# Cross attention: the sample tokens' steps placed behind products of the next head, and the norm factors' spread placed between the halves of the first gate product

## Chip, cores and metric

The kernel runs on one core of one Trainium2 chip. The metric is the device time of one execution in microseconds (us), the median over the runs of one session.

## The reference, cut to what matters

One layer of a streaming encoder works on 1024 prompt tokens and 64 sample tokens, side by side in one token axis of T = 1088. The part that the change touches is the cross attention, with 4 heads of width 256 and 256 memory tokens, and the step after it:

```python
def cross_attn(x, mk, mv, g_cross, w_cq, w_co):
    q = (rms_norm(x, g_cross) @ w_cq).reshape(B, S, MEM_HEADS, MEM_HD)
    s = jnp.einsum('bqhd,bkhd->bhqk', q, mk) * (MEM_HD ** -0.5)
    p = jax.nn.softmax(s, axis=-1)
    o = jnp.einsum('bhqk,bkhd->bqhd', p, mv)
    return o.reshape(B, S, MEM_HEADS * MEM_HD) @ w_co
# prompt tokens: mk, mv from this call's memory; sample tokens: from a cache
hp = hp + cross_attn(hp, mk, mv, ...);  hs = hs + cross_attn(hs, cache_mem_k, cache_mem_v, ...)
h  = h + (silu(rms_norm(h) @ w_gate) * (rms_norm(h) @ w_up)) @ w_down
```

## The kernel before, in words

Nearly every product is made of three matmuls (`mm3`, lines 157 to 159): both operands are split into a rounded high part and a remainder (`split`: ScalarE casts the high part, line 124, VectorE subtracts, line 125). The tensor engine (PE) works through products of this kind almost without a gap; VectorE (DVE), ScalarE (ACT), GpSimd (POOL) and the DMA queue of SyncE (SP) prepare operands and take results.

The program is written as a list of operations in Python, and a scheduler that estimates durations puts each engine's instructions into a fixed order. `issue_after(x)` holds an operation back until instruction x in that order; `in_order(f)` runs f so that its instructions stand behind the last matmul issued so far. `self.later` is a list of functions that `run_later` empties; `dense`, the helper for one product of a weight unit with a token chunk, calls `run_later` at its end.

`cross_phase` loops over the 4 heads (`attend`). For each head and each of the four token chunks in `CQ` (256, 256, 256 and 320 columns) it makes two query products (`pd<-xc,wq`, 24 matmuls each), scales them by the norm factor (`qf`), splits them (`cqs`), makes the scores (`css`, 12 matmuls), a softmax on DVE and ACT (`small_softmax`; names `cnm`, `cden`, `p`), four transposes (`cpt`), a split of these (`cpT`) and 12 matmuls with the values (`cpo`), whose result is split into the tile `co`. The last chunk holds the 64 sample tokens; their queries go to `qsm`. After the four chunks of a head come the sample tokens' own steps, with the cache's keys `ck` and values `cv`: scores `csss` (line 1355, 2 matmuls, 4 records in the trace), softmax into `ps`, two transposes `cpts` (line 1360), a copy `cpTs` (line 1362) and 4 matmuls `cpos` (line 1366, 8 records in the trace), split into the last 64 columns of `co`. These matmuls and the transposes take plain fp32 operands and are not split into three. PSUM has 3 banks for dense products, 2 for scores (`s`), 1 for transposes (`t`), 2 for `cpo` and `cpos` (`o`); the SBUF tag `t2` has 4 buffers for `mraw`, `qf`, `p`, `ck`, `cv` and `ps`.

`cross_out_phase` then multiplies `co` with `w_co` (`pd<-co,wq`; chunks `CH` of 384, 384 and 320 columns), adds the stored residual (`hx`, line 1394) and keeps sums of squares. At its end the norm factors of two of the three chunks are left to the start of the feed-forward: `self.later` then holds `spread_both` (line 369: 6 fp32 matmuls of a factor row with the identity, then two ACT copies into `rstd_f`, line 372).

The feed-forward begins with `gate_up`. Its first gate product is made by `plain`: four result blocks of 544 columns by 2x128 rows, each of two halves `part(i, t, 0)` and `part(i, t, 1)`, each half 24 matmuls. Three first halves, then `early()` (the last factors' roots), then the three second halves, then `run_later`, then the results are taken by `emit` (which needs `rstd_f`), then both halves of the fourth block. A block holds one of 4 PSUM bank pairs, and so does the spread.

Of the kernel before, what the change touches and what calls it, by code (L numbers as in the profile page):

```python
# [11 lines left out]
F32 = mybir.dt.float32  # L12
# [7 lines left out]
P = 128  # L20
D = 1024
KT = D // P
SEQ = 1024
SMP = 64
T = SEQ + SMP
CH = ((0, 384), (384, 384), (768, 320))
CQ = ((0, 256), (256, 256), (512, 256), (768, 320))
BLK = 256
NBLK = SEQ // BLK
H = 4  # L30
# [79 lines left out]
class Kernel:  # L110
# [132 lines left out]
    def plain(self, w, x, emit, early=None, second=None):  # L243

        ps = {}
        def part(i, t, j):
            if j == 0:
                ps[i, t] = self.bank_pair()
            return self.multiply(ps[i, t], w[i, j], x[f"B{j + 1}{t + 1}"], j == 0, j == 1)

        for i, t in ((0, 0), (1, 0), (0, 1)):
            part(i, t, 0)
        if early is not None:
            with self.tc.issue_after(self.last_mm):
                early()
        emits = [(0, 0), (1, 0), (0, 1)]
        out = []
        for i, t in emits:
            out.append(part(i, t, 1))
            if second is not None and len(out) == 1:  # L260
                second(emit(i, t, out[0], None))
        with self.tc.issue_after(self.last_mm):
            self.run_later()
        for (i, t), o in list(zip(emits, out))[second is not None:]:
            emit(i, t, o, None)
        part(1, 1, 0)
        emit(1, 1, part(1, 1, 1), None)
# [1016 lines left out]
    def cross_phase(self):  # L1284
        nc, tc, io = self.nc, self.tc, self.io
        mm = nc.tensor.matmul
        with ExitStack() as ctx:
            cp = ctx.enter_context(tc.tile_pool(name="cp", bufs=1, reuse_waits="tile"))
            pc = ctx.enter_context(tc.tile_pool(name="pc", bufs=1, reuse_waits="tile", space=PSUM))
            self.norm_psum = lambda name: pc.tile([P, 512], F32, tag="t", name=name)  # L1290
            t2 = lambda name: cp.tile([P, 2, 256], F32, tag="t2", bufs=4, name=name)
            outs = [None] * H

            def small_softmax(ps, rows, units, p):
                nm = cp.tile([P, 2], F32, tag="nm", bufs=2, name="cnm")
                den = cp.tile([P, 2], F32, tag="den", bufs=2, name="cden")
                nc.vector.tensor_reduce(nm[:rows, :units], ps[:rows, :units, :], AX.X, ALU.max)
                nc.vector.tensor_scalar(nm[:rows, :units], nm[:rows, :units], -1.0 / 16, None, ALU.mult)
                for i in range(units):
                    nc.scalar.activation(p[:rows, i, :], ps[:rows, i, :], AF.Exp, bias=nm[:rows, i:i + 1], scale=1.0 / 16,  # L1300
                                         accum_out=den[:rows, i:i + 1])
                nc.vector.reciprocal(den[:rows, :units], den[:rows, :units])
                for i in range(units):
                    nc.vector.tensor_scalar(p[:rows, i, :], p[:rows, i, :], den[:rows, i:i + 1], None, ALU.mult)

            def attend(h):
                us = [self.unit(io["w_cq"][2 * h + i], KT) for i in range(2)]
                hl = []
                for src in (self.d_mk, self.d_mv):
                    raw = t2("mraw")  # L1310
                    self.load(raw, src[h])
                    s = cp.tile([P, 2, 2, 256], F32R, tag=f"m{len(hl)}", bufs=1, name="mkv")
                    self.split(raw, s[:, 0], s[:, 1])
                    hl.append(s)
                mk, mv = hl
                outs[h] = self.ring_tiles(1, 2, "co")
                for c0, n in CQ:
                    ps = [self.dense(us[i], self.xs, c0, n) for i in range(2)]
                    qf = t2("qf")
                    for i in range(2):  # L1320
                        nc.vector.tensor_tensor(out=qf[:, i, :], in0=ps[i][:, :256], in1=self.rstd[:, c0:c0 + 256], op=ALU.mult)
                    qs = cp.tile([P, 2, 2, 256], F32R, tag="qs", bufs=2, name="cqs")
                    self.split(qf, qs[:, 0], qs[:, 1])
                    if n > 256:
                        qsm = cp.tile([P, 2, SMP], F32, tag="qsm", bufs=1, name="qsm")
                        for i in range(2):
                            nc.vector.tensor_tensor(out=qsm[:, i, :], in0=ps[i][:, 256:n], in1=self.rstd[:, SEQ:T], op=ALU.mult)
                    pss = pc.tile([P, 2, 256], F32, tag="s", bufs=2, name="css")
                    for t in range(2):
                        for dt in range(2):  # L1330
                            q = qs[:, :, dt, t * P:(t + 1) * P]
                            self.mm3(pss[:, t, :], q[:, 0], q[:, 1], mk[:, 0, dt, :], mk[:, 1, dt, :], dt == 0, dt == 1)
                    p = t2("p")
                    small_softmax(pss, P, 2, p)
                    pt = pc.tile([P, 2, 256], F32, tag="t", bufs=1, name="cpt")
                    for kt in range(2):
                        for t in range(2):
                            nc.tensor.transpose(pt[:, kt, t * P:(t + 1) * P], p[:, t, kt * P:(kt + 1) * P], self.ident)
                    pT = cp.tile([P, 2, 2, 256], F32R, tag="pT", bufs=1, name="cpT")
                    self.split(pt, pT[:, 0], pT[:, 1])  # L1340
                    po = pc.tile([P, 2, 256], F32, tag="o", bufs=2, name="cpo")
                    for dt in range(2):
                        dd = slice(dt * P, (dt + 1) * P)
                        for kt in range(2):
                            self.mm3(po[:, dt, :], mv[:, 0, kt, dd], mv[:, 1, kt, dd], pT[:, 0, kt, :], pT[:, 1, kt, :],
                                     kt == 0, kt == 1)
                    for dt in range(2):
                        o = outs[h][dt]
                        self.split(po[:, dt, :], o[:, 0, c0:c0 + 256], o[:, 1, c0:c0 + 256])
                ck, cv = t2("ck"), t2("cv")  # L1350
                self.load(ck, io["cmkT"][h])
                self.load(cv, io["cmv"][h])
                pss = pc.tile([P, 2, 256], F32, tag="s", bufs=2, name="csss")
                for dt in range(2):
                    mm(pss[:SMP, 0, :], qsm[:, dt, :], ck[:, dt, :], start=dt == 0, stop=dt == 1)
                p = t2("ps")
                small_softmax(pss, SMP, 1, p)
                pt = pc.tile([P, 2, 256], F32, tag="t", bufs=1, name="cpts")
                for kt in range(2):
                    nc.tensor.transpose(pt[:, kt, :SMP], p[:SMP, 0, kt * P:(kt + 1) * P], self.ident[:SMP, :SMP])  # L1360
                pT = cp.tile([P, 2, SMP], F32, tag="pTs", bufs=1, name="cpTs")
                nc.vector.tensor_copy(pT, pt[:, :, :SMP])
                po = pc.tile([P, 2, 256], F32, tag="o", bufs=2, name="cpos")
                for dt in range(2):
                    for kt in range(2):
                        mm(po[:, dt, :SMP], cv[:, kt, dt * P:(dt + 1) * P], pT[:, kt, :], start=kt == 0, stop=kt == 1)
                for dt in range(2):
                    o = outs[h][dt]
                    self.split(po[:, dt, :SMP], o[:, 0, SEQ:T], o[:, 1, SEQ:T])

            for h in range(H):
                attend(h)
            self.couts = sum(outs, [])
# [219 lines left out]
    def turn(self, name, group):  # L1593

        if name == "T4":
            self.slots["B12"] = self.slots["T4"]
            name = "B12"
        if name[0] == "B":
            self.load_operand(name, group)
# [302 lines left out]
```

## Time and profile before

| | |
|---|---|
| time, median of 3 runs | 2162.29 us (2162.05 to 2165.18) |
| the profiled execution's own time | 2162.52 us |
| its span in the profile | 2160.7 us |
| PE busy | 2134.5 us, 99% of the span |
| DVE, ACT, POOL busy | 1552.6, 874.8, 530.4 us |
| DMA | 290.85 MB, 135 GB/s on average |

A row of the timeline gives an instruction's start and its duration in us, engine, source line, operation, result tile and operands, size, a count when equal ones follow each other, and in brackets the idle time of the engine just before it with what ended it. Matmuls overlap: the time that one takes from the next is the difference of their starts, called its slot here.

### The profile page before, as it was taken

Reading aid. Unit: us, or ns where it says so; the run is one execution under the profiler, and the core shown is the slowest. Engines: PE = TensorE matmul, PEld = TensorE weight load, DVE = VectorE, ACT = ScalarE, POOL = GpSimd, SP = SyncE. Lnnn points to the kernel's source line nnn. Section 1 sums busy time; section 2 is a strip of 40 time slices with the busy share of each in tenths; the row PEclk is TensorE's granted clock in tenths of the full one; section 3 lists DMA queues with packets and bytes.
Section 4 is the critical chain, followed back from the end, with each engine's and each line's share of the span. In section 5 each row is a group of like instructions: output and inputs, shape, how many; then the busy total and the mean of one; then the engine's idle time right before and its main releaser. Section 6 shows DMA issues by size and latency. Waiting matters only on the chain.

```text
span 2160.7 us, 41729 instructions
## 1 busy us (share of the span) xinstructions
PE 2134.5 (99%) x16371; PEld 2082.7 (96%) x16371; DVE 1552.6 (72%) x2912; ACT 874.8 (40%) x1894; POOL 530.4 (25%) x448
## 2 busy tenths in 40 slices
PE   9999999999999999999999999999999999999997
PEld 9999999999999997889999999999999999999997
DVE  8987979776677567656455555677777777777597
ACT  8344434344444356543233333343223222334243
POOL 0000000022343135540000000015565556423531
PEclk9999999999999999999999999999999999999998
DMA  7334444435345485336442122413342332484333
GB/s 262 126 126 123 129 145 134 128 114 160 113 140 190 158 260 184 120 116 207 142 142 78 50 64 68 145 58 105 123 147 91 101 132 82 132 298 158 106 116 113
DMA packets 169893, 290.85 MB, mean 135 GB/s; under 512 B 39266, under 2 KB 96546, under 8 KB 169698
## 3 DMA queue, kind: packets, MB, share of 16 engines
q1 hardware_dynamic: 161666, 269.02, 38.8%
q0 software_dynamic: 3424, 10.82, 1.4%
q10 hardware_dynamic: 4608, 8.36, 1.0%
q8 instruction: 129, 2.11, 0.4%
q14 instruction: 66, 0.54, 0.1%
HBM read 196.97 MB, written 91.16 MB: 133 GB/s over the span
## 4 chain that ended last, share of the span: by engine, by line
PE 85%; DVE 7%; DMA 3%; issue 2%; ACT 2%; POOL 1%; SPq 0%; POOLq 0%; DVEq 0%; ACTq 0%
PE pq L226 17%; PE pq L224 16%; PE pq L223 16%; PE pd L157 8%; PE pd L159 8%; PE pd L158 8%; DVE wq L125 2%; DMA hl<-d_op 1%; PE pss L1005 1%; PE pout L1075 1%; DVE T L125 1%; PE pk L766 1%; PE pp L1051 1%; DVE B L125 1%; PE po L159 1%
## 5 line engine op out<-in xcount | busy, mean ns | idle before, releaser
L124 ACT CAST wq<-raw 128x512 fp32r<-128x512 f32 (+1 forms) x499 | 302.0, 614 | 564.7 <-PE pq L226 220.1
L125 DVE TENSOR_TENSOR wq<-raw,wq 128x512 fp32r<-128x512 f32 (+1 forms) x499 | 426.6, 859 | 137.3 <-ACT wq L124 133.9
L224 PE MATMUL pq<-T,wq 128*128 128x272 f32 x1832 | 492.1, 288 | 0.5 <-DVE T L125 0.5
L223 PE MATMUL pq<-T,wq 128*128 128x272 f32 x1832 | 490.4, 287 | 1.6 <-ACT wq L124 0.6
L224 PE MATMUL pq<-B,wq 128*128 128x272 f32 x1592 | 427.3, 288 | 1.9 <-DVE B L125 1.9
L223 PE MATMUL pq<-B,wq 128*128 128x272 f32 x1592 | 425.6, 287 | 0.2 <-ACT B L124 0.2
L226 PE MATMUL pq<-T,wq 128*128 128x272 f32 x1832 | 382.7, 289 | 1.9 <-DVE wq L125 1.9
L201 POOL TENSOR_TENSOR raw<-raw 128x512 f32<-128x512 f32 (+1 forms) x44 | 62.9, 1429 | 1260.5 <-DVE wq L125 527.6
L223 PEld LDWEIGHTS pq<-T,wq 128*128 128x128 f32 x1832 | 344.3, 188 | 3.2 <-ACT xsq L499 1.2
L224 PEld LDWEIGHTS pq<-T,wq 128*128 128x128 f32 x1832 | 343.9, 188 | 1.5 <-issue 0.7
L226 PE MATMUL pq<-B,wq 128*128 128x272 f32 x1592 | 331.9, 289 | 0.0
L224 PEld LDWEIGHTS pq<-B,wq 128*128 128x128 f32 x1592 | 298.9, 188 | 3.4 <-DVE B L125 3.0
L223 PEld LDWEIGHTS pq<-B,wq 128*128 128x128 f32 x1592 | 298.9, 188 | 0.7 <-ACT B L124 0.4
L226 PEld LDWEIGHTS pq<-T,wq 128*128 128x128 f32 x1832 | 289.6, 189 | 3.6 <-DVE wq L125 2.4
L226 PEld LDWEIGHTS pq<-B,wq 128*128 128x128 f32 x1592 | 251.7, 189 | 0.9 <-issue 0.7
L274 DVE TENSOR_TENSOR u<-pq,u 128x544 f32<-128x544 f32 x177 | 127.1, 718 | 76.0 <-PE pq L226 75.5
L613 DVE TENSOR_TENSOR stage<-pq,u 128x544 f32<-128x544 f32 x112 | 80.1, 717 | 32.5 <-PE pq L226 26.7
L157 PE MATMUL pd<-xc,wq 128*128 128x256 f32 (+1 forms) x256 | 74.5, 291 | 0.0
L159 PE MATMUL pd<-xc,wq 128*128 128x256 f32 (+1 forms) x256 | 74.0, 289 | 0.0
L158 PE MATMUL pd<-xc,wq 128*128 128x256 f32 (+1 forms) x256 | 73.7, 288 | 0.0
L1550 POOL TENSOR_TENSOR stage<-stage,rstd_f 128x544 f32<-128x544 f32 x40 | 63.9, 1608 | 39.1 <-ACT stage L1549 39.1
L204 POOL TENSOR_TENSOR raw<-raw 128x512 f32<-128x512 f32 (+1 forms) x44 | 59.0, 1340 | 53.1 <-DVE wq L125 50.5
(388 smaller groups left out, 4508.9 us busy)
## 6 DMA issues: line engine op xcount, KB each, us to landing
hl<-d_op SPq DMA_DIRECT2D x85, 272.0 KB, 5.3
d_qkv<-stage SPq DMA_DIRECT2D x44, 272.0 KB, 2.3
d_op<-stage SPq DMA_DIRECT2D x44, 272.0 KB, 2.2
d_op<-ht SPq DMA_DIRECT2D x44, 272.0 KB, 3.3
raw<-w_gate SPq DMA_DIRECT2D x22, 512.0 KB, 3.5
raw<-w_up SPq DMA_DIRECT2D x22, 512.0 KB, 5.0
raw<-w_down SPq DMA_DIRECT2D x16, 512.0 KB, 4.8
d_gate<-stage ACTq DMA_DIRECT2D x28, 272.0 KB, 2.8
```

The source lines that it names most:

```text
L124: self.last_cast = self.nc.scalar.copy(hi, src).ins
L125: return self.nc.vector.tensor_tensor(out=lo, in0=src, in1=hi.bitcast(F32), op=ALU.subtract).ins
L157: mm(ps, wh, xh, start=start, stop=False)
L158: mm(ps, wh, xl, start=False, stop=False)
L159: self.last_mm = mm(ps, wl, xh, start=False, stop=stop).ins
L201: tt(out=a11, in0=a11, in1=a21, op=sub)
L223: mm(ps[:, c, :HC], w[:, 0, ks], x[:, 0, cs], start=start, stop=False)
L224: mm(ps[:, c, :HC], w[:, 0, ks], x[:, 1, cs], start=False, stop=False)
L226: self.last_mm = mm(ps[:, c, :HC], w[:, 1, ks], x[:, 0, c * HC:(c + 1) * HC], start=False, stop=stop).ins
L274: add = lambda out, a, b: nc.vector.tensor_tensor(out=out, in0=a, in1=b, op=ALU.add)
L613: nc.vector.tensor_tensor(out=o, in0=ps, in1=sb, op=ALU.add)
L1550: nc.gpsimd.tensor_tensor(out=g, in0=g, in1=r[t], op=ALU.mult)
```

## The change

The sample tokens' steps of a head no longer follow its four chunks. `sample` is called in the chunk that holds the sample tokens, loads `ck` and `cv` into tags of their own with one buffer each (`ps` has one too), and puts the scores into `self.later`; they are issued behind the next dense product, and append the transposes behind the one after it, and those append the products with `cv` behind the third. For heads 0 to 2 these are products of the next head. In the last head the chunk of 320 columns comes first, so that they are products of its own later chunks.

In `plain`, when `early` is given, `run_later` runs after the second of the three second halves, not after the third.

```diff
@@ plain
         for i, t in emits:
             out.append(part(i, t, 1))
+            if early is not None and second is None and len(out) == 2:
+                with self.tc.issue_after(self.last_mm):
+                    self.run_later()
@@ cross_phase
+            def sample(h, qsm):
+                ck, cv, p = (cp.tile([P, 2, 256], F32, tag=t, bufs=1, name=t) for t in ("ck", "cv", "ps"))
+                self.load(ck, io["cmkT"][h])
+                self.load(cv, io["cmv"][h])
+
+                def scores():
+                    pss = pc.tile([P, 2, 256], F32, tag="s", bufs=2, name="csss")
+                    for dt in range(2):
+                        mm(pss[:SMP, 0, :], qsm[:, dt, :], ck[:, dt, :], start=dt == 0, stop=dt == 1)
+                    small_softmax(pss, SMP, 1, p)
+                    behind(turn)
+
+                def turn():
+                    pt = pc.tile([P, 2, 256], F32, tag="t", bufs=1, name="cpts")
+                    for kt in range(2):
+                        nc.tensor.transpose(pt[:, kt, :SMP], p[:SMP, 0, kt * P:(kt + 1) * P], self.ident[:SMP, :SMP])
+                    pT = cp.tile([P, 2, SMP], F32, tag="pTs", bufs=1, name="cpTs")
+                    nc.vector.tensor_copy(pT, pt[:, :, :SMP])
+                    behind(lambda: weigh(pT))
+
+                def weigh(pT):
...
+                behind = lambda f: self.later.append(lambda: self.in_order(f))
+                behind(scores)
@@ attend
-                for c0, n in CQ:
+                for c0, n in CQ if h < H - 1 else CQ[3:] + CQ[:3]:
...
                     if n > 256:
...
+                        sample(h, qsm)
...
-                ck, cv = t2("ck"), t2("cv")
-                self.load(ck, io["cmkT"][h])
-                self.load(cv, io["cmv"][h])
...
```

`weigh` holds the four matmuls with `cv` and the split into `co`; the lines removed at the end of `attend` are the same steps in a row.

In the program's order, first PE where head 0 ends. Before, the transposes and the products with `cv` stand together between the last products with the values (`cpo`) and the next head's query products (`pd<-xc`):

```order
L158 MATMUL cpo<-cpT,mkv 128x256
L159 MATMUL cpo<-cpT,mkv 128x256
L1360 MATMUL cpts<-ident,ps 128x64 x2
L1366 MATMUL cpos<-cpTs,cv 128x64 x4
L157 MATMUL pd<-xc_13007,wq 128x256
```

Now the transposes stand alone, then come other products, and the four matmuls with `cv` are parted by the eleven other matmuls of the next chunk's `cpo`:

```order
L159 MATMUL cpo<-cpT,mkv 128x256
L1324 MATMUL cpts<-ident,ps 128x64 x2
L158 MATMUL pd<-xc_13008,wq 128x256
...
L157 MATMUL cpo<-cpT,mkv 128x256
L1333 MATMUL cpos<-cpTs,cv 128x64 x3
L158 MATMUL cpo<-cpT,mkv 128x256
...
L159 MATMUL cpo<-cpT,mkv 128x256
L1333 MATMUL cpos<-cpTs,cv 128x64
L158 MATMUL pd<-xc_13013,wq 128x256
```

Between the transposes and the first of the products stand more than 50 matmuls of other work; the scores `csss` moved up from between the transposes `cpt` of the head's last chunk to among its scores.

Second, PE where the last head ends (`co0`, `co1` with the highest numbers are this head's two result tiles, `pd_15994` is the first product of the second row block of `w_co`). Before, the sample steps are followed by six matmuls of the first row block's chunk of 320 columns:

```order
L159 MATMUL cpo_15813<-cpT_15810,mkv_15406 128x256
L1360 MATMUL cpts_15845<-ident_63,ps_15837 128x64 x2
L1366 MATMUL cpos_15850<-cpTs_15848,cv_15831 128x64 x4
L157 MATMUL pd_15955<-co0_15409,wq_15888 128x320
L158 MATMUL pd_15955<-co0_15409,wq_15888 128x320
L159 MATMUL pd_15955<-co0_15409,wq_15888 128x320
L157 MATMUL pd_15955<-co1_15410,wq_15888 128x320
L158 MATMUL pd_15955<-co1_15410,wq_15888 128x320
L159 MATMUL pd_15955<-co1_15410,wq_15888 128x320
L157 MATMUL pd_15994<-co0_13962,wq_15986 128x384
```

Now six matmuls of the chunk of columns 384 to 767 stand directly behind the last prompt chunk's `cpo`:

```order
L159 MATMUL cpo_15842<-cpT_15839,mkv_15382 128x256
L157 MATMUL pd_15924<-co0_15385,wq_15888 128x384
L158 MATMUL pd_15924<-co0_15385,wq_15888 128x384
L159 MATMUL pd_15924<-co0_15385,wq_15888 128x384
L157 MATMUL pd_15924<-co1_15386,wq_15888 128x384
L158 MATMUL pd_15924<-co1_15386,wq_15888 128x384
L159 MATMUL pd_15924<-co1_15386,wq_15888 128x384
L157 MATMUL pd_15994<-co0_13962,wq_15986 128x384
```

The sample steps are gone from this place; the six matmuls behind it read a piece of `co` that was now written last.

Third, the loads on SP for heads 0 and 1. Before, the cache's keys and values of head 0 come after two weight loads, and the next head's keys and values (`mraw`) behind them:

```order
L118 DMA mraw<-d_mk 128x512
L118 DMA mraw<-d_mv 128x512
L118 DMA raw<-w_cq 128x1024 x2
L118 DMA ck<-cmkT 128x512
L118 DMA cv<-cmv 128x512
L118 DMA mraw<-d_mk 128x512
L118 DMA mraw<-d_mv 128x512
```

Now head 0's stand ahead of the weight loads, and `ck` of head 1 stands ahead of head 1's `mraw`; having one buffer, it waits there for head 0's `csss`:

```order
L118 DMA mraw<-d_mk 128x512
L118 DMA mraw<-d_mv 128x512
L118 DMA ck<-cmkT 128x512
L118 DMA cv<-cmv 128x512
L118 DMA raw<-w_cq 128x1024 x2
L118 DMA ck<-cmkT 128x512
L118 DMA mraw<-d_mk 128x512
L118 DMA mraw<-d_mv 128x512
L118 DMA cv<-cmv 128x512
```

So a load that head 1 needs for its first scores is queued behind one that waits for PE.

More of the change, by code (lines that the diff above doesn't have):

```diff
@@ L1304, in small_softmax @@
                     nc.vector.tensor_scalar(p[:rows, i, :], p[:rows, i, :], den[:rows, i:i + 1], None, ALU.mult)
+            def sample(h, qsm):
[16 more added lines that the diff above has]
+                def weigh(pT):
+                    po = pc.tile([P, 2, 256], F32, tag="o", bufs=2, name="cpos")
+                    for dt in range(2):
+                        for kt in range(2):
+                            mm(po[:, dt, :SMP], cv[:, kt, dt * P:(dt + 1) * P], pT[:, kt, :], start=kt == 0, stop=kt == 1)
+                    for dt in range(2):
+                        o = outs[h][dt]
+                        self.split(po[:, dt, :SMP], o[:, 0, SEQ:T], o[:, 1, SEQ:T])
+                behind = lambda f: self.later.append(lambda: self.in_order(f))
+                behind(scores)
             def attend(h):
@@ L1349, in attend @@
                         self.split(po[:, dt, :], o[:, 0, c0:c0 + 256], o[:, 1, c0:c0 + 256])
-                ck, cv = t2("ck"), t2("cv")
-                self.load(ck, io["cmkT"][h])
-                self.load(cv, io["cmv"][h])
[L1353 to L1369, printed above, removed]
             for h in range(H):
```

## Prediction

> **What bounds the kernel now.** PE is busy nearly throughout the span (the table above), so only what PE does, or what it waits for, can move the time. I asked first who PE waits for in the cross attention from head 0's last chunk to the first output product, and how much idle time there is:
>
> ```profile
> PE cpos L1366 <- DVE cpTs L1362: 1.7, 4, 0.6
> PE cpo L157 <- ACT cpT L124: 0.7, 1, 0.7
> PE cpo L158 <- DVE cden L1302: 0.3, 1, 0.3
> PE pd L157 <- ACT co L124: 0.3, 1, 0.3
> 1207.00:1346.00 139.00, 135.88 (x1046) 130.92 (x1045) 77.85 (x200) 52.48 (x143) 0.00 (x0) 1.00 0.17 54
> ```
>
> The columns are total, times and longest; in the last row, window, length, then busy time of PE, weight loads, DVE, ACT, POOL, and the granted clock. PE misses 3.1 us of 139, all at the sample steps or right behind them; DVE and ACT are half free and the clock is full. So at most some microseconds of 2162 are on offer. Idle time counts from the modelled end of a matmul; I use slots (start to next start). First the slots where nothing waits:
>
> ```profile
> 1185.73 0.49 PE L1338 MATMUL cpt<-ident,p 128*128 128x128 f32 x3
> 1185.97 0.36 PE L158 MATMUL css<-mkv,cqs 128*128 128x256 f32 x1
> 1186.17 0.28 PE L157 MATMUL pd<-xc,wq 128*128 128x256 f32 x1
> 1186.29 0.28 PE L158 MATMUL pd<-xc,wq 128*128 128x256 f32 x1
> ```
>
> Three transposes take 0.24 us (0.08 each), a 256-column matmul 0.12, but 0.20 as the first one behind plain fp32 work: leaving such a block costs 0.08. I scale 0.12 with the columns: 0.15 for 320, 0.18 for 384.
>
> **Waits that go.** Head 0 is the worst, since no query product stands between its last transposes and `cpo`:
>
> ```profile
> 1214.23 0.55 PE L1338 MATMUL cpt<-ident,p 128*128 128x128 f32 x3
> 1215.51 0.39 PE L157 MATMUL cpo<-cpT,mkv 128*128 128x256 f32 x1 [0.73 <-ACT cpT L124]
> 1216.23 0.39 PE L158 MATMUL cpo<-cpT,mkv 128*128 128x256 f32 x1 [0.34 <-DVE cden L1302]
> 1216.46 0.28 PE L159 MATMUL cpo<-cpT,mkv 128*128 128x256 f32 x1
> 1217.74 0.34 PE L1360 MATMUL cpts<-ident,ps 64*128 64x64 f32 x2
> 1218.65 1.10 PE L1366 MATMUL cpos<-cpTs,cv 128*128 128x64 f32 x8 [0.58 <-DVE cpTs L1362]
> 1219.57 0.36 PE L157 MATMUL pd<-xc,wq 128*128 128x256 f32 x1
> ```
>
> Slots against normal: transposes 1.28 for 0.24 (1.04 lost), first `cpo` 0.72 for 0.20 (0.52), second 0.23 for 0.12 (0.11), `cpts` 0.91 for two transposes, 0.17 (0.74). Sum 2.41 us. The eight `cpos` records take 0.92. Head 1 stands for heads 1 to 3:
>
> ```profile
> 1253.65 0.49 PE L1338 MATMUL cpt<-ident,p 128*128 128x128 f32 x3
> 1254.07 1.08 PE L1355 MATMUL csss<-ck,qsm 128*64 128x256 f32 x4
> 1255.08 0.38 PE L157 MATMUL pd<-xc,wq 128*128 128x256 f32 x1
> 1255.30 0.28 PE L158 MATMUL pd<-xc,wq 128*128 128x256 f32 x1
> 1257.89 0.28 PE L159 MATMUL cpo<-cpT,mkv 128*128 128x256 f32 x1
> 1258.10 0.33 PE L1360 MATMUL cpts<-ident,ps 64*128 64x64 f32 x2
> 1258.81 1.10 PE L1366 MATMUL cpos<-cpTs,cv 128*128 128x64 f32 x8 [0.38 <-DVE cpTs L1362]
> ```
>
> `cpts` takes 0.71 for 0.17: 0.54 lost, three times 1.62. In the new order some 26 matmuls (3 us) stand between `cpt` and `cpo` of head 0, and more than 50 (6 us) between `cpts` and `cpos`, against a wait that is over within 1.3 us of the first transpose. All 4.03 us go.
>
> **What is late next: the end of the last head.**
>
> ```profile
> 1340.74 0.28 PE L159 MATMUL cpo<-cpT,mkv 128*128 128x256 f32 x1
> 1340.95 0.34 PE L1360 MATMUL cpts<-ident,ps 64*128 64x64 f32 x2
> 1341.67 1.10 PE L1366 MATMUL cpos<-cpTs,cv 128*128 128x64 f32 x8 [0.38 <-DVE cpTs L1362]
> 1344.42 0.44 PE L157 MATMUL pd<-co,wq 128*128 128x384 f32 x1
> 1344.70 0.34 PE L158 MATMUL pd<-co,wq 128*128 128x384 f32 x1
> 1342.39 0.42 DVE L125 TENSOR_TENSOR co<-cpo,co 128x256 fp32r<-128x256 f32 x1 [0.44 <-ACT co L124]
> 1343.80 1.08 DVE L1394 TENSOR_TENSOR hx<-pd,hx 128x384 f32<-128x384 f32 x2
> ```
>
> Before, `cpos` (0.92), leaving (0.08) and six matmuls of 320 columns (0.90) would bring the next product to 1343.57; it came at 1344.42, 0.62 after the first `hx` began, which frees its bank, and its slot is 0.28 for 0.18: 0.95 lost. So 4.98 us are lost in all. After, the sample steps are away, but the last prompt chunk's `co` is what the six matmuls read, and in DVE's queue `hx` still stands behind it. The last DVE part of `co` ended 2.07 us after the last `cpo` began (1342.39 + 0.42 - 1340.74); then 0.01 to `hx` and 0.62 from there to PE: the next product comes 2.70 us after that `cpo`, where 0.12 and six times 0.18 would make 1.20. 1.50 and the restart's 0.10 are lost: 1.60. The wait is not removed there, it changes its owner. Net of waits: 4.98 - 1.60 = 3.38 us.
>
> **What the split blocks cost.** Before, `csss` stood against the transposes and `cpts` against `cpos`. Now, by the order, they make 5, 3 and 8 blocks of their own (one `cpts` joins a `cpos`) and head 0's transposes two instead of one: 13 more exits. Behind `csss` the exit is 0.10 (0.22 for 0.12), behind the others 0.08: 1.04 to 1.30, I take 1.17. Entering: before, the transposes ahead of `csss` took 0.42 for 0.25, four times 0.17, and `cpts` was entered at 0.21 for 0.12, four times 0.09: 1.04. After, `cpts` three times 0.09; `csss` from a split product is not in the trace: between 0 (as `cpt`) and 0.17, I take 0.09 as for `cpts`, its nearest row, 64 wide too; `cpos` between 0 and 0.09, I take 0 as for `cpt`, which is also 128 wide. That is 0.72 (0.27 to 1.84): 0.32 less than before (0.77 less to 0.80 more). Cross attention: 3.38 - 1.17 + 0.32 = 2.53 us gained (1.28 to 3.11).
>
> The row behind fp32 work says 0.20 for 0.12. The Trainium skill ("TensorE: Matmul & The Clock Gate", "Step-by-step: what each phase is for") says that PE's queue pulls the next weight load ahead of running matmuls, so that the two overlap. By that rule a block's edge need cost nothing, and this sum would be 3.4 to 4.4; the trace does not agree at these edges, and the row decides.
>
> **The spread in the first gate product.** The fourth block's bank is the one that the spread gives back, through two ACT copies:
>
> ```profile
> 1443.85 0.16 DVE L329 TENSOR_TENSOR rs_r<-rs_r,root 128x3 f32<-128x3 f32 x1
> 1446.13 0.29 PE L223 MATMUL pq<-B,wq 128*128 128x272 f32 x1
> 1449.12 1.50 PE L369 MATMUL pq<-ident,rs_r 128*128 128x128 f32 x12
> 1451.51 0.39 PE L223 MATMUL pq<-b,wq 128*128 128x272 f32 x1 [0.90 <-ACT rstd_f L372]
> 1451.74 0.29 PE L224 MATMUL pq<-b,wq 128*128 128x272 f32 x1
> 1177.75 0.83 PE L361 MATMUL pb<-ident,rs_r 128*128 128x128 f32 x6
> 1178.33 0.36 PE L157 MATMUL css<-mkv,cqs 128*128 128x256 f32 x1
> ```
>
> The third second half starts at 1446.13; the spread now stands there. The factors are ready at 1444.01, so it need not wait, and the half behind it (3 us) covers the copies. Six such matmuls took 0.58 elsewhere, twelve 1.17, and 0.20 with the exit: 1.37 for the 2.62 from 1449.12 to 1451.74. Gain 1.25, at least the idle 0.90. If that cover were gone, the 0.90 would be back. In DVE's queue the remainder of a weight of the up product (line 125) stands some operations later than before; its user on PE comes behind the fourth block and two products of up.
>
> **Moved loads.** `ck` and `cv` have buffers of their own now, and on SP each `ck` waits for the previous head's `csss`, with the next head's `mraw` behind it; `cv` waits for the previous `cpos`. Their users stand 6 us or more behind those in the order, against these landing times (first `mraw`, then `cv`):
>
> ```profile
> DMA to landing us min/median/max: 2.5/2.8/4.2
> DMA to landing us min/median/max: 4.0/4.0/5.6
> ```
>
> 4.2, and a 0.6 us cast, still fit: cost 0. The same matmuls, copies and bytes remain.
>
> **Sum.** 2.53 + 1.25 = 3.78 us (2.2 to 4.4) off the profiled execution's 2162.52 gives 2158.7; its own time is 0.2 above the median 2162.29, so 2158.5 against that. From there on the work hangs on `hx`, as before, so the gain should reach the end.
>
> **Rivals.** (1) The edges are free, since the next weights load behind running matmuls: 4.98 - 1.60 + 1.25 = 4.63, up to 5.67 if the 1.04 of entries before goes too: 2157.7 to 2156.6, taken at 2157.2. This is what the rule of the Trainium skill's page on TensorE, above, would make of the time. For it: the entry of `cpt` costs nothing. Against: every first matmul behind fp32 work in this stage takes 0.20.
>
> (2) The gain is given back downstream, by a chain that had just enough time. DVE, third behind the window's length, is full around the gate product:
>
> ```profile
> 1448.00:1458.00 10.00, 9.10 (x75) 8.91 (x74) 10.00 (x15) 7.17 (x12) 1.81 (x2) 1.00 0.00 0
> ```
>
> If DVE sets the pace there, the 1.25 goes, and half of the rest: 2161.0. Against: PE waits in that window for ACT alone, and DVE's moved operations have later users.
>
> (3) Slower: the next head's keys arrive late, as `mraw` stands behind the waiting `ck`. Three heads can pay. With 6 us between `csss` and the first scores, 0.6 for the cast, and 4.2 to land, there is 1 us to spare; each us beyond costs PE a us per head. To be slower by 0.2% (4.3 us) it has to eat 3.8 as well, 2.7 per head: a landing of 8 us, where the longest here is 5.6. It would then be about 2167.
>
> (4) The change doesn't do what it says: excluded, the order shows all of it.
>
> **How the numbers follow.** About 0.2%, 4.3 us, is what a measurement of this kernel can tell from no change: faster begins below 2158.0. Forecast 0.54, at 2158.5, its own range 2157.9 to 2160.1, just on the near side of that line; rival 1 0.30; rival 2 0.10; rival 3 0.06. Of the forecast's cases I put 0.08 over the line: faster 0.38, same 0.56, slower 0.06. The range goes from 2156.9, which leaves out the last of rival 1, to rival 2's 2161.0.
>
> **What would show it.** Right: no PE wait at `cpos` or `cpo` in heads 0 to 2; one wait of about 1.5 us between the last `cpo` and the second row block, ended by DVE's `hx` or ACT's `co`; first matmuls behind the new blocks at 0.20 to 0.22; no idle time before the fourth gate block. Wrong: PE waiting for `mkv` or `ck`; a tail without a wait; new idle time behind the gate product.

## The result, and the profile after

| | before | after |
|---|---|---|
| median of 12 runs each | 2161.82 us | 2157.74 us |
| ratio, 95% interval | | 0.9984 (0.9976 to 0.9991) |
| profiled execution, its span | 2162.52, 2160.7 | 2156.32, 2154.5 |

The change makes the kernel faster by 0.16% (0.09 to 0.24): 3.5 us by the ratio, where the two medians alone differ by 4.1. That is less than the 0.2% that the prediction called the line. The median is 0.8 us under the predicted 2158.5, of which 0.5 is that before itself came out at 2161.82, not 2162.29.

The total is a coarse measure here, since single executions of one kernel spread over 7 us. Stages of one execution are a fine one. I use four points on PE: P, the six matmuls `pt` ahead of the cross attention; S, the first product of the second row block of `w_co`; G, the first gate matmul; F, the second matmul of the fourth gate block. The timeline of before has P and G at

```profile
1172.05 0.73 PE L337 MATMUL pt<-ones,rstd 128*128 128x2 f32 x6
1430.49 0.29 PE L223 MATMUL pq<-B,wq 128*128 128x272 f32 x1
```

and that of after at

```profile
1172.72 0.73 PE L340 MATMUL pt<-ones,rstd 128*128 128x2 f32 x6
1428.87 0.29 PE L223 MATMUL pq<-B,wq 128*128 128x272 f32 x1
```

So P to G is 258.44 before and 256.15 after. With S (1344.42 and 1342.79) P to S is 172.37 and 170.07, 2.30 less; with F (1451.74 and 1448.97, below) G to F is 21.25 and 20.10, 1.15 less. Together 3.45 us. Of the 6.2 us between the two profiled executions the rest isn't shown to be the change's: after reached P 0.67 us later, in code that is the same, and gained 3.4 behind F, where before waits 1.9 us for split operands (`B`) whose loads came late, and after doesn't. The code behind F is the same too, and that part took 705.1 to 709.0 us in the executions traced here.

The waits of PE in after, from head 0's last chunk to the first output product (total, times, longest), and the busy row of that window:

```profile
PE pd L157 <- ACT co L124: 0.5, 1, 0.5
PE pd L157 <- DVE qf L1356: 0.4, 1, 0.4
1207.00:1346.00 139.00, 138.12 (x1062) 133.41 (x1062) 76.98 (x202) 53.82 (x146) 0.00 (x0) 1.00 0.18 56
```

All waits at `cpos` and `cpo` are gone, and PE misses 0.9 us where it missed 3.1. Two waits are new. The first is the foreseen tail; the timeline of PE and DVE there:

```profile
1340.27 0.28 PE L159 MATMUL cpo<-cpT,mkv 128*128 128x256 f32 x1
1341.01 0.44 PE L157 MATMUL pd<-co,wq 128*128 128x384 f32 x1 [0.46 <-ACT co L124]
...
1342.79 0.44 PE L157 MATMUL pd<-co,wq 128*128 128x384 f32 x1
1343.07 0.34 PE L158 MATMUL pd<-co,wq 128*128 128x384 f32 x1
1341.85 0.42 DVE L125 TENSOR_TENSOR co<-cpo,co 128x256 fp32r<-128x256 f32 x1 [0.44 <-ACT co L124]
1342.19 0.55 DVE L1410 TENSOR_TENSOR hx<-pd,hx 128x384 f32<-128x384 f32 x1
```

From the last `cpo` to S are 2.52 us for 1.20: 1.32 lost, and 0.10 in the restart's slot. The second was not foreseen. In the last head, the first product of `w_co` needs the bank that `qf` frees, and on DVE the maximum of the scores (1322.10), the splits of `cpo` and of `cpos`, and the split of a weight (`wq`) stand ahead of that `qf`. The last timeline row is ACT's cast of the same weight:

```profile
1323.65 0.28 PE L159 MATMUL pd<-xc,wq 128*128 128x256 f32 x1
1324.31 0.44 PE L157 MATMUL pd<-co,wq 128*128 128x384 f32 x1 [0.38 <-DVE qf L1356]
...
1323.04 0.21 DVE L125 TENSOR_TENSOR co<-cpos,co 128x64 fp32r<-128x64 f32 x1
1323.24 0.68 DVE L125 TENSOR_TENSOR wq<-raw,wq 128x512 fp32r<-128x512 f32 x1
1323.84 0.42 DVE L1356 TENSOR_TENSOR qf<-pd,rstd 128x256 f32<-128x256 f32 x1
1322.57 0.62 ACT L124 CAST wq<-raw 128x512 fp32r<-128x512 f32 x1 [0.32 <-PE pd L159]
```

The slot is 0.66 for 0.12 and the restart costs 0.10: 0.64 us lost. The sample step's own split is not what holds `qf` up: it takes 0.13 of DVE's queue (1323.04 to 1323.17), and the weight's split behind it, 0.60 from start to start, needs the cast that ended at 1323.19, so without the split of `cpos` it could have begun 0.05 earlier at most.

The gate in after, PE's timeline, and the busy row behind it:

```profile
1444.51 1.50 PE L372 MATMUL pq<-ident,rs_r 128*128 128x128 f32 x12
1445.76 0.37 PE L223 MATMUL pq<-B,wq 128*128 128x272 f32 x1
1445.97 0.29 PE L224 MATMUL pq<-B,wq 128*128 128x272 f32 x1
...
1448.85 0.29 PE L223 MATMUL pq<-b,wq 128*128 128x272 f32 x1
1448.97 0.29 PE L224 MATMUL pq<-b,wq 128*128 128x272 f32 x1
1448.00:1458.00 10.00, 10.00 (x83) 10.00 (x82) 10.00 (x16) 7.16 (x11) 3.29 (x2) 1.00 0.00 0
```

The fourth block follows without a wait. DVE is now full for these 10 us (third number behind the window's length), and PE still never waits for it.

The keys of the last head: the load is issued behind the waiting `ck`, split on DVE, and first used on PE:

```profile
1288.57 0.42 SPq L118 DMA_DIRECT2D mraw<-d_mk  x1
1292.19 0.69 DVE L125 TENSOR_TENSOR mkv<-mraw,mkv 128x512 fp32r<-128x512 f32 x1 [1.73 <-ACT mkv L124]
1297.20 0.28 PE L157 MATMUL css<-mkv,cqs 128*128 128x256 f32 x1
```

They are ready 4.3 us before their use.

### The profile page after: what moved, and what is told of

It is laid out like the page before. It is cut to its first block, busy times and chain, and to the rows that moved or that the text cites. A ratio compares the mean times of both kernels' runs of the same rounds, so it can differ in the third digit from the quotient of the medians.

```text
span 2154.5 us, 41702 instructions
## 1 busy us (share of the span) xinstructions
PE 2133.1 (99%) x16371; PEld 2082.9 (97%) x16371; DVE 1550.4 (72%) x2912; ACT 875.0 (41%) x1894; POOL 531.9 (25%) x448
## 4 chain that ended last, share of the span: by engine, by line
PE 88%; DVE 5%; issue 2%; DMA 2%; ACT 2%; POOL 1%; SPq 0%; POOLq 0%; DVEq 0%; ACTq 0%
PE pq L226 18%; PE pq L223 17%; PE pq L224 17%; PE pd L157 8%; PE pd L158 8%; PE pd L159 8%; DVE wq L125 1%; PE pout L1078 1%; PE pss L1008 1%; PE pk L769 1%; DVE T L125 1%; PE pp L1054 1%; PE po L158 1%; PE po L159 1%; PE po L157 1%
```

## Experiments

All stage times are of one profiled execution each; the changed kernel's second execution (below) tells what they are worth.

| kernel | P to S | P to G | G to F | median | ratio to before |
|---|---|---|---|---|---|
| before | 172.37 | 258.44 | 21.25 | | |
| after | 170.07 | 256.15 | 20.10 | 2157.74 | 0.9984 (0.9976 to 0.9991) |
| after, second execution | 170.08 | 256.14 | 20.11 | | |
| spread alone | 172.35 | 258.42 | 20.10 | 2159.04 | 0.9991 (0.9980 to 1.0002) |
| own buffers, early loads | 169.47 | 254.48 | 21.26 | 2157.05 | 0.9981 (0.9971 to 0.9990) |
| own buffers alone | 169.48 | 254.63 | 21.29 | | |
| after, residual early | | 253.78 | 20.14 | 2156.13 | 0.9974 (0.9964 to 0.9984) |
| after, `cpos` in one block, twice | 170.09, 170.09 | 255.10, 255.25 | 20.10, 20.14 | | |
| after, 32 matmuls more | 178.40 | 263.56 | 20.13 | | |
| buffers, residual, spread | | 253.18 | 20.13 | 2154.99 | 0.9979 (0.9970 to 0.9988) |
| the same, `csss` whole in all heads | | 254.19 | 20.10 | 2155.50 | 0.9987 (0.9978 to 0.9995) |
| the same, `csss` whole in heads 0 to 2 | | 252.65 | 20.10 | 2153.24 | 0.9977 (0.9967 to 0.9986) |

Where the second row block starts ahead of the last `co`, S has no counterpart. Each ratio is to runs of before on the same chip. Apart from before, a row without a median is of single executions.

**The changed kernel again.**

> The changed kernel a second time, for what a stage's time is worth. In three runs so far (before, after, the spread alone) a matmul of 384 columns in the output projection took 0.1767 us from its start to the next, in the three others 0.1733, and the whole projection 1.05 us less. If that is the kernel's own, it is 0.1767 again and the stage up to the gate 256.15; if it belongs to the execution, it may be 0.1733 and 255.1. The part up to the second row block of the projection should be 170.07 again within 0.05, the gate stage 20.10.

Every stage came back within 0.01 us, and the 384-column matmuls took 0.1767 again. Up to S the kernel with whole `cpos` blocks (below) repeated as well. So I take a difference of 0.1 us between two kernels up to S as the kernels'. From S to G it isn't always; see the last section.

**The spread alone.** Before, with

```diff
             out.append(part(i, t, 1))
+            if early is not None and second is None and len(out) == 2:
+                with self.tc.issue_after(self.last_mm):
+                    self.run_later()
```

> The kernel before with the move in the first gate product alone. I measure two stages on PE: from the norm factors' six matmuls ahead of the cross attention (pt) to the first gate matmul (258.44 us before, 256.15 after), and from there to the second matmul of the fourth gate block (21.25 before, 20.10 after). My theory: the two parts are independent, so the first stage stays at 258.4 and the second falls to 20.1 (1.15 less; the prediction said 1.25), and no new idle time on PE follows behind the fourth block; in the total about 1.1 us less, which a measurement can't tell from nothing. Rival, given back downstream: the second stage falls, but new idle time of up to 1.15 us stands behind the fourth block.

As expected: 258.42 and 20.10, and no new idle time behind the block; the total can't tell it from nothing. The two parts of the change are independent, and the gate's 1.15 is not given back. That is the end of the prediction's rival 2 for this part.

**Own buffers.** Before, with only

```diff
                     if n > 256:
...
+                        ck, cv, psm = (cp.tile([P, 2, 256], F32, tag=t, bufs=1, name=t) for t in ("ck", "cv", "ps"))
+                        self.load(ck, io["cmkT"][h])
+                        self.load(cv, io["cmv"][h])
...
-                ck, cv = t2("ck"), t2("cv")
-                self.load(ck, io["cmkT"][h])
-                self.load(cv, io["cmv"][h])
...
-                p = t2("ps")
```

> The kernel before, with no step moved by the code: ck, cv and ps have only tags of their own and the two loads stand at the head's chunk with the sample tokens, as after. The spread is as before. Theory A, the shared buffers and late loads held the sample steps at the head's end, and the scheduler places them by itself once they are free: its order now has 26 or more other matmuls between cpts and cpos in heads 0 to 2 and joins cpos to the next transposes, so of the waits 2.41 + 2 x 0.54 = 3.49 go; 36 plain fp32 blocks instead of 33 cost 0.27: the stage up to the gate goes from 258.44 to about 255.2 (254.9 to 255.6), more than the whole change gained there. The last head's wait at cpos (0.4 us idle) and its late first row block (0.95) stay. Theory B, it is the queue of functions in the code that removes the waits: then this kernel keeps the waits at cpos, and the stage stays at 258.4 (257.9 if head 0's first scores move alone).

Theory A holds. Up to S it gains 2.90 us, more than the whole change does there (2.30), and in heads 0 to 2 PE's timeline has the steps 3.3 us apart and no wait (head 1):

```profile
1263.93 0.33 PE L1359 MATMUL cpts<-ident,ps 64*128 64x64 f32 x2
...
1267.24 1.00 PE L1365 MATMUL cpos<-cpTs,cv 128*128 128x64 f32 x8
```

The last head's waits stayed, as expected. Up to G the stage, 254.48, came out below the stated 254.9 to 255.6. The gain to S is at the low edge of what was expected (2.9 to 3.5); the rest of its 3.96 up to G lies between S and G, where nothing was changed (last section).

**Own buffers alone.** The loads stay at their old place:

```diff
-                ck, cv = t2("ck"), t2("cv")
+                ck, cv, psm = (cp.tile([P, 2, 256], F32, tag=t, bufs=1, name=t) for t in ("ck", "cv", "ps"))
...
-                p = t2("ps")
```

> The kernel before with nothing changed but the tags of ck, cv and ps: three buffers of their own instead of three turns of the four shared ones; the loads stay where they stood in the code. In the order the sample steps stand on PE as in the run with own buffers and early loads. If the shared buffers alone held the steps, the stage up to the gate is 254.5 (254.3 to 254.7) as there, against 258.44 before; if the early loads matter, PE waits at csss, by some tenths per head.

The same up to S within 0.01. So what held the sample steps at the end of heads 0 to 2 was that `ck`, `cv` and `ps` took turns with the operands of the next head in four shared buffers. With buffers of their own the scheduler moves the steps by itself.

**The residual early.** After, with the first three `hx` in a small pool that is opened ahead of the cross attention:

```diff
-                x = cq.tile([P, 384], F32, tag="hx", bufs=4, name="hx")[:, :n]
+                x = (self.hxp if m == 0 else cq).tile([P, 384], F32, tag=f"hx{c0}" if m == 0 else "hx", bufs=1 if m == 0 else 4, name="hx")[:, :n]
```

> The changed kernel with the first three residual pieces hx of the output projection in a small pool of their own, so that their loads and additions don't wait for memory of the cross attention; in the order the additions of two pieces now stand ahead of the last co split on DVE, and 22 matmuls of the second row block stand between the last cpo and the six matmuls that wait for co. My theory: the tail's loss in the changed kernel (2.52 us from the last cpo to the second row block, for 1.20, and 0.1 at the restart, 1.42 in all) has its place in these two queues and goes: the stage up to the gate falls from 256.15 to 254.7 (254.6 to 255.0). Rival: a PSUM bank is still late, by another owner, and a wait of 0.5 to 1.4 us stays there (255.2 to 256.1).

PE goes from the last `cpo` straight into the second row block, since on DVE two `hx` now stand ahead of the last `co` (the first began at 1339.73):

```profile
1341.88 0.28 PE L159 MATMUL cpo<-cpT,mkv 128*128 128x256 f32 x1
1342.00 0.34 PE L157 MATMUL pd<-co,wq 128*128 128x384 f32 x1
1340.89 0.56 DVE L1413 TENSOR_TENSOR hx<-pd,hx 128x384 f32<-128x384 f32 x1
1342.60 0.43 DVE L125 TENSOR_TENSOR co<-cpo,co 128x256 fp32r<-128x256 f32 x1 [0.49 <-ACT co L124]
```

4 us behind the last `cpo`, where both orders have joined, it is 1.45 us ahead of after: the tail's 1.42, shown. The other 0.9 of its gain up to G comes bit by bit from there on, in the unchanged stretch; it brings the stage to 253.78, below the stated 254.6 to 255.0.

**Whole `cpos` blocks.** After, with

```diff
-                    for dt in range(2):
-                        for kt in range(2):
-                            mm(po[:, dt, :SMP], ...)
+                    with self.tc.high_priority():
+                        for dt in range(2):
+                            for kt in range(2):
+                                mm(po[:, dt, :SMP], ...)
```

> The changed kernel with the four cpos matmuls of a head kept together (in the changed kernel they stand as three and one with eleven other matmuls between): 41 plain fp32 blocks in the cross attention instead of 44, nothing else moved. Theory, leaving a block costs 0.08 to 0.10 us: the stage up to the gate falls by 0.24 to 0.30, to 255.9. Rival 1 of the prediction, edges are free: 256.15.

Up to S nothing: 170.09, in both executions. Up to G it took 1.05 and 0.90 us less, all of it behind S, where the order is the same (last section). The theory of a price per exit falls. Its rows of PE against those of after, first after:

```profile
1267.55 0.28 PE L157 MATMUL cpo<-cpT,mkv 128*128 128x256 f32 x1
1267.67 0.78 PE L1333 MATMUL cpos<-cpTs,cv 128*128 128x64 f32 x6
1268.25 0.36 PE L158 MATMUL cpo<-cpT,mkv 128*128 128x256 f32 x1
1268.45 0.27 PE L159 MATMUL cpo<-cpT,mkv 128*128 128x256 f32 x1
...
1269.65 0.33 PE L1333 MATMUL cpos<-cpTs,cv 128*128 128x64 f32 x2
1269.79 0.36 PE L159 MATMUL css<-mkv,cqs 128*128 128x256 f32 x1
```

then the whole block:

```profile
1272.66 1.00 PE L1334 MATMUL cpos<-cpTs,cv 128*128 128x64 f32 x8
1273.47 0.36 PE L158 MATMUL cpo<-cpT,mkv 128*128 128x256 f32 x1
```

Each plain matmul is two records. Six records take 0.58, two 0.14, eight 0.81, and each time the next slot is 0.08 too long: 0.66, 0.22 and 0.89, that is 0.22 a matmul and nothing for the block. The long slot at the exit is the end of the block's own work, and the block's first matmul is shorter by as much.

**32 blocks more.** After, with this in `dense`, asked for by the query products alone:

```diff
+        if extra:
+            with self.tc.issue_after(self.last_mm), self.tc.high_priority():
+                for _ in range(extra):
+                    self.nc.tensor.matmul(ps[:, 448:512], self.ident, self.ident[:, :64], start=True, stop=True)
         self.run_later()
```

> The changed kernel with one more plain fp32 matmul (identity, 64 columns, the form of cpos; its result is never read) behind each of the 32 query products: 32 such matmuls, and 25 more blocks in the order. The disputed cost by itself: in a block of four, a cpos matmul took 0.20 us and the exit 0.08. Theory of the prediction, every exit costs 0.08: 32 x 0.28 = 9.0 us more (0.20 and 0.08 each). Rival 1, in the form that the run with whole cpos blocks suggests (a block of 1, 3 and 4 matmuls with its exit took 0.22, 0.67 and 0.89, 0.22 each and nothing for the edge): 32 x 0.22 = 7.0 more. Measured up to the second row block of the projection, 170.07 in the changed kernel.

The rows say it directly:

```profile
1188.17 0.33 PE L169 MATMUL pd<-ident 128*128 128x64 f32 x2
1188.31 0.36 PE L157 MATMUL pd<-xc,wq 128*128 128x256 f32 x1
1188.51 0.28 PE L158 MATMUL pd<-xc,wq 128*128 128x256 f32 x1
```

0.14 and 0.08 too much behind: 0.22, as rival 1 has it. The stage alone would not have told: it grew by 8.33, between the two expectations, since a new wait of PE for `cpT` in the last head takes some 1.45 of it (slots of 0.97, 0.73 and 0.22 for 0.23, 0.12 and 0.12), the wait for `qf` went (0.64), and one more head has its two `csss` parted (0.34, below). The 7.2 left are 0.23 for each of the 31 that stand behind P.

**Buffers, residual and spread together.** Before, with the edits of three runs above: own buffers and early loads, the residual early, the spread alone. No step is placed by the code.

> The kernel before with own buffers for ck, cv and ps (as in the run with own buffers alone), the early residual pieces and the spread's move, and no step placed by the code. In its order cpos of the last head stands behind a part of the second and third row blocks. Theory: the last head's losses, 0.56 at cpts and 0.95 at the first row block, go as well: the stage up to the gate is 254.48 - 1.5 = 253.0 (252.7 to 253.5, if a 384-column matmul takes 0.1733 as there, 1.05 more if 0.1767), the gate stage 20.1; in the total 2155 against 2157.7 of the changed kernel, about 6 below before. Rival: the scheduler's new order opens a wait of its own at the last head (the last co, or a bank): 254.0 or more.

253.18, and PE has no wait at all from P to G. In the total it is 0.21% under before. The 253.18 lies in the stated range, and the 384-column matmuls took the 0.1733 that it assumed.

**`csss` whole.** The same, with

```diff
-                for dt in range(2):
-                    mm(pss[:SMP, 0, :], qsm[:, dt, :], ck[:, dt, :], start=dt == 0, stop=dt == 1)
+                with tc.high_priority():
+                    for dt in range(2):
+                        mm(pss[:SMP, 0, :], qsm[:, dt, :], ck[:, dt, :], start=dt == 0, stop=dt == 1)
```

> The kernel with buffers, residual and spread, and the two csss matmuls of a head kept together; the other one parts them in two of four heads. By the rows so far, a block with one csss matmul costs 0.77 us (0.09 in the slot ahead, 0.58, 0.10 behind), one with two 1.20, so parting them costs 0.34: theory, the stage up to the gate is 0.68 shorter than in the other kernel, 252.3. Rival, the edges are free for this form too: the same within 0.1. The order around the scores moves a little with it, so a new wait there of some tenths is possible.

Slower by 1.0 up to G instead of faster by 0.68. The partings went, but the last head's order moved with them, and PE waits there again:

```profile
PE pd L157 <- DVE hx L1400: 0.6, 1, 0.6
PE pd L157 <- ACT co L124: 0.3, 1, 0.3
```

**`csss` whole in heads 0 to 2.** The same with

```diff
-                with tc.high_priority():
+                with tc.high_priority() if h < H - 1 else nullcontext():
```

> The kernel with own buffers, early residual and the spread, and the two csss matmuls kept together in heads 0 to 2 alone, so that the last head's order stays as in the kernel with buffers and residual (253.18 us up to the gate), where heads 0 and 2 part them. Theory: two partings of 0.34 each go and no wait comes: 252.5 (252.4 to 252.8). Rival, parting costs nothing in the end because something else waits instead: 253.2.

252.65, and no wait from P to G: 0.53 less than with two heads parted, where 0.68 was expected. A parted pair, of the kernel with buffers and residual, and a whole one, of this kernel:

```profile
1285.57 0.28 PE L158 MATMUL css<-mkv,cqs 128*128 128x256 f32 x1
1285.78 0.65 PE L1361 MATMUL csss<-ck,qsm 128*64 128x256 f32 x2
1286.36 0.39 PE L158 MATMUL cpo<-cpT,mkv 128*128 128x256 f32 x1
```

```profile
1282.99 0.28 PE L157 MATMUL css<-mkv,cqs 128*128 128x256 f32 x1
1283.20 1.08 PE L1362 MATMUL csss<-ck,qsm 128*64 128x256 f32 x4
1284.20 0.39 PE L158 MATMUL cpo<-cpT,mkv 128*128 128x256 f32 x1
```

One matmul takes 0.09 ahead (0.21 for 0.12), 0.58, and 0.10 behind (0.22 in after, and in the prediction's row): 0.77. Two take 0.09, 1.00 and 0.10: 1.19. In this form a block's edges do cost, about 0.35. It is no matter of plain fp32 against split products: beside the transposes `cpt`, in before, a pair costs 1.20 as well (0.17, 1.01 and 0.10, less the 0.08 behind `cpt`).

The weight loads (PEld) show where the two forms differ. The first load of `cpos` in after starts with the matmul ahead of it, 0.12 before its own; that of `csss`, here in the kernel of this run, starts with its own matmul:

```profile
1267.55 0.75 PEld L1333 LDWEIGHTS cpos<-cpTs,cv 128*128 128x128 f32 x6
1283.19 0.62 PEld L1362 LDWEIGHTS csss<-ck,qsm 128*64 128x64 f32 x4
```

The load of the product behind `csss` starts with its matmul too, at 1284.20. In after this is so at every edge of `csss` and of `cpts`, whose weights fill 64 of 128 columns or rows (`128*64`, `64*128`): the load starts within 0.01 us of its matmul. At those of `cpos` and `cpt`, both `128*128`, it starts ahead, by 0.09 to 0.15 on entering and 0.02 to 0.03 on leaving. That the width of 64 is the reason is not shown, since no run changed it alone.

This version is 0.23% under before and the best here by the stages; by the totals the changed kernel with the residual early (0.26%) can't be told from it. Against after it is 3.5 us less from P to F (272.75 to 276.25), some 1 us of which is the unchanged stretch's; the totals' intervals overlap, so that it beats after is shown by the stages, not by the totals.

## Why the prediction was right, and where not

- **Waits removed.** Right: those at `cpos` and `cpo` are gone in all heads, by the waits of after. What had held the steps the prediction didn't ask; in heads 0 to 2 it was the shared buffers, and the code's queue isn't needed there.
- **The tail.** Right in place and owner; 1.42 lost where 1.60 was forecast, as S came 2.52 us behind the last `cpo`, not 2.70. The run with the residual early shows that the loss was DVE's order.
- **The step that failed: "All 4.03 us go."** They went, but in the last head's new order the first product of `w_co` came before DVE had freed its bank with a `qf`, and 0.64 came back. The prediction looked for a late bank in the tail alone and put nothing for one inside the last head, since DVE looked half free. The rows put most of the delay on what every chunk and product brings (the maximum, the splits of `cpo` and of a weight), not on the moved steps. The wait is missing in the runs that keep the last head's old order, and also in the one with 32 matmuls more; which operation would have to move is not tested.
- **The blocks.** The forecast was 1.17 for exits less 0.32 for entries, 0.85 in all. Up to S, where the restart's 0.10 doesn't count yet, 4.88 of waits less 1.32 and 0.64 would be 2.92; 2.30 was gained, so the blocks cost 0.62. The size is near, the reason wrong: the exit of `cpos` and `cpt` is no price, as rival 1 said. `cpt` is linear as well, since one transpose takes 0.03 and 0.08 behind it, three take 0.24 and 0.08. What costs is `csss` (0.34 where head 0's two matmuls were parted, worked out from rows), and `cpts` was mis-sized. In after its two transposes take 0.26, not 0.17, and leave 0.11 behind them, not 0.08:

```profile
1221.88 0.33 PE L1324 MATMUL cpts<-ident,ps 64*128 64x64 f32 x2
1222.14 0.39 PE L158 MATMUL pd<-xc,wq 128*128 128x256 f32 x1
1222.37 0.28 PE L159 MATMUL pd<-xc,wq 128*128 128x256 f32 x1
```

Before, they stood against `cpos` and made nothing late behind them, so the 0.09 and the 0.11 are 0.20 a head; one `cpts` now stands against a `cpos`, which saves an entry of 0.09: 0.71 in all. Against this, `cpos` no longer starts behind a wait: with what is late behind them its four matmuls take 0.89, where 0.92 and 0.08 made 1.00 before, 0.44 less in four heads. So 0.34, 0.71 and -0.44 make 0.61 of the 0.62, as far as rows of single blocks can tell. The number was off too: by the order there are 11 more blocks, not 13, because of fewer blocks of `cpt`.
- **The rule of the Trainium skill** ("TensorE: Matmul & The Clock Gate", "Step-by-step: what each phase is for"), that the next weights load behind running matmuls, was set aside in the prediction for the 0.20 slots. The runs agree with it for `cpos` and `cpt`: 0.22 a `cpos` matmul in any block, and the first load 0.12 ahead. For `csss` and `cpts` they don't: their loads start with their own matmul, and leaving them costs 0.10 to 0.11.
- **The gate.** 1.15 for 1.25: twelve spread matmuls took 1.25 us, where twice the six's 0.58 made 1.17, and the exit 0.09 for 0.08.
- **Moved loads.** Right at 0, with 4.3 us to spare; rival 3 did not come. Rival 2 did not either: 10 full microseconds of DVE behind the gate delayed nobody.
- **Sum.** 3.78 forecast, 3.45 by the stages, 3.5 (1.9 to 5.2) by the ratio. That they are so near is partly luck: against the forecast stand 0.64 for `qf` and 0.10 at the gate, for it 0.18 in the tail and 0.23 in the blocks, and nothing in the prediction made these cancel.

## What to carry to other kernels

When a step waits in a place where other work is at hand, ask first which buffer keeps the scheduler from moving it; three buffer names did more here than the code that places the steps. When the order changes, take each product that moved forward, and look which copy frees its bank and what stands ahead of that copy on its engine. A long slot behind a block of another kind is a price only if the block doesn't begin early by as much: compare blocks of different lengths and look when the weight loads start before counting edges. Where the total is noisier than the effect, compare stages between fixed points of two traces.

## What the hardware showed that was not expected

From S to G all these kernels issue nearly the same products, and yet this stretch takes 86.07 us in before, 86.08 in after and 85.01 in the first execution with whole `cpos` blocks. The time is in the matmuls of 384 columns: 0.1767 us from start to start against 0.1733, while those of 320 columns take 0.1467 in both. The groups of one line between 1350 and 1410 us show it, first after:

```profile
L157 PE MATMUL pd<-co,wq 128*128 128x384 f32 x81 | 27.4, 339 | 0.0
```

then whole `cpos` blocks:

```profile
L157 PE MATMUL pd<-co,wq 128*128 128x384 f32 x82 | 27.5, 336 | 0.0
```

It can change within an execution. In the second execution with whole blocks the slower value held for some 8 us behind S, then the faster one, which makes the 0.15 us between its 255.25 and 255.10. Expected on record for it was 255.10 again, if the value is the kernel's, or 256.15, if it is the execution's; it was neither. Before, after (twice) and the spread alone kept the slower value until the last few microseconds of these matmuls. The granted clock was 1.00 in either case. What sets it is open; up to 1.05 us of a stage's time hang on it, so gains up to G were read from S where they could be.
